# Attention on one core: a weave that starts with the second query tile, first rows loaded in f32 by the hardware queues, and a new order in the last period

## The chip, the core and the metric

The kernel runs on one core of a Trainium2 chip. The metric is the device time of one execution in microseconds (us), lower is better. A profile shows the span from the first to the last instruction, which is about 2 us shorter than the device time of the same execution. All runs quoted here were in the fast state, with a mean granted TensorE clock (its share of full speed) of 0.994 to 1.000. Single executions of one kernel still scatter by a few us, so medians are given with the lowest and highest run.

Engines: PE does the matmuls, DVE and ACT work on vectors, POOL issues the casting loads (the "software queue"), and SP issues stores and transposing transfers (a "hardware queue"; ACT can issue to one too). PSUM is the memory that takes the results of PE, in banks. "Landed" means that all bytes of a transfer have arrived.

## The reference

```python
# q, k, v: (8, 2048, 512) float32
scores = np.matmul(q, k.transpose(0, 2, 1)) / np.sqrt(d_k)
attn_weights = special.softmax(scores, axis=-1).astype(np.float32)
return np.matmul(attn_weights, v)
```

## The kernel before

A batch has four query tiles of 512 queries, so there are 32 tiles. Inputs are cast to f16 during the load. Both matrix products use a scheme with seven block products instead of eight (Winograd's form of Strassen's method). It needs sums of blocks, which DVE computes ("k sums", "q sums", "v sums", "p sums"). In matmuls of 256 columns, a score tile costs 112 this way and 128 when plain. The values of a tile cost 112.

In the steady loop a period (28 steps, called slots) weaves the scores of tile g+1 with the values of tile g on PE. A short queue of pending sums, `background`, is worked off in certain slots. DVE works in the order in which the instructions were written, and every sum is an instruction in that order.

```python
def prefetch(g, slot):                 # steady loop: loads, transposes, sums of later tiles
    ...
        elif what[0] == "trans":
            dma_transpose(what[1], bb, c)      # a transposing transfer, issued by SP
        else:
            background.extend({"k": k_sums, "q": q_sums, "v": v_sums}[what[1]](bb, c))
    if background and slot % len(QORDER) in (0, 2, 3, 6):
        background.popleft()()
```

Before the loop, tiles 0 and 1 are computed plainly, with the values of tile 0 put in late:

```python
load("q", 0, 0, 2); load("k", 0, 0, 2)         # software queue, f32 -> f16 on the way
load("k", 0, 1);    load("k", 0, 2)
...                                            # 14 dummy matmuls, first transposes on PE
for kb in range(NKB):
    plain_tile(0, kb)
    ...
load("q", 0, 2); load("q", 0, 3)
pe_transpose("q", 0, 1)
p_sums(0, NG - 1)
for kb in range(NKB):
    plain_tile(1, kb)
    if kb == 3: dma_transpose("q", 0, 2)
    if kb == 4: dma_transpose("q", 0, 3)
    ...                                        # v sums, p sums, first values of tile 0
for n in range(4, len(ORDER)):
    pv(0, n)                                   # the other values of tile 0, with k and q sums
    ...
for g in range(1, NP + 1):                     # the steady loop, first scores: tile 2
    ...
```

Each pair of output rows (`Pair`, letters a and b) goes through seven products. ACT scales a product into the output (`scaled`) and DVE adds to it (`final`). The pair's three PSUM banks are then free for the next pair. Lines are cut where "..." stands.

The softmax here doesn't subtract the row's maximum and nothing guards it: scores larger than these inputs give would overflow.

Of the kernel before, what the change touches and what calls it, by code (L numbers as in the profile page):

```python
# [12 lines left out]
def kernel(  # L13
# [21 lines left out]
    nc = tc.nc  # L35
# [49 lines left out]
    nc.sync.dma_start(out=ident[:], in_=ident_dram.ap())  # L85
# [12 lines left out]
    def load(what, b, c, pieces=1):  # L98
        t = stage.tile([P, CH, D], F16, tag="stage")
        w = CH // pieces  # L100
        for n in range(0, CH, w):
            at = c * CH + n
            nc.gpsimd.dma_start(out=t[:, n:n + w, :], in_=srcs[what][b, :, at:at + w, :])  # L103
        staged[what, b, c] = t
# [16 lines left out]
    def pe_transpose(what, b, c):  # L121
        src = staged.pop((what, b, c))
        t = operands(what)
        for n in range(0, CH, 2):
# [6 lines left out]
            nc.vector.tensor_copy(out=t[0][:, n:n + 2], in_=tr[:])  # L131
        (kT if what == "k" else qT)[b, c] = t
# [83 lines left out]

    class Group:
# [69 lines left out]
    def p_sums(g, n, part=None):  # L287
# [4 lines left out]
        if part in (None, 0):  # L292
            add(s1[:, js], a21, a22)  # L293
            sub(s2[:, js], s1[:, js], a11)  # L294
            sub(a21, a11, a21)
        if part in (None, 1):
            sub(s4[:, js], a12, s2[:, js])  # L297

    class Pair:
# [6 lines left out]
        def product(self, n):  # L306
# [3 lines left out]
            cols = slice(i * P, (i + 1) * P)  # L310
            if n == 1:
                self.x = bank("px")
            elif n == 2:
                self.y = bank("py")
            elif n == 5:
                self.z = bank("pz")
# [29 lines left out]
        def store(self, o, half):  # L346
            b, qt = divmod(self.g, NQT)
            n = qt * NQS + half * (NQS // 2) + self.i
            nc.sync.dma_start(out=out[b, n * P:(n + 1) * P, :], in_=o[:])
# [27 lines left out]
        def after7(self):  # L377
            self.final(self.o2[:, H:D], self.x[:, 0:H], self.r2)

        def after4(self):  # L380
            self.scaled(self.o2[:, 0:H], self.x[:, 0:H], self.r2)
            self.store(self.o2, 1)
# [30 lines left out]
    def prefetch(g, slot):  # L413
        b, qt = divmod(g, NQT)
        todo = PLAN.get((qt, slot), [])
        if g == 1:
            todo = [x for x in PLAN.get((0, slot), ()) if x[0] == "newv" or x[1] == "v"] + todo
        for what in todo:
            bb, c = b + 1, what[-1]
            if what[0] != "newv" and what[1] == "q":  # L420
                if not NQT <= g + what[2] < B * NQT:
                    continue
# [11 lines left out]
        if background and slot % len(QORDER) in (0, 2, 3, 6):  # L434
            background.popleft()()

# [4 lines left out]
    def pv(g, n):  # L441
        which = ORDER[n]
        g -= which.endswith("'")
        if g < 0:
            return
# [6 lines left out]
    load("q", 0, 0, 2)  # L452
    load("k", 0, 0, 2)
    load("k", 0, 1)
    load("k", 0, 2)

    dummy = bank("qy")
    for n in range(14):
        nc.tensor.matmul(dummy[:], warm[:, 0:P], warm[:], start=True, stop=True)
    pe_transpose("q", 0, 0)  # L460
    pe_transpose("k", 0, 0)
    new_v(0)
    load("k", 0, 3)
    load("q", 0, 1)
    for kb in range(NKB):
        plain_tile(0, kb)
        if kb % CH == 1 and kb // CH + 1 < NCH:
            pe_transpose("k", 0, kb // CH + 1)
        if kb % (2 * G) == 0 and kb:
            p_sums(0, kb // (2 * G) - 1)  # L470
        if kb % CH == 3:
            load_v(0, kb // CH)
    load("q", 0, 2)
    load("q", 0, 3)
    pe_transpose("q", 0, 1)
    p_sums(0, NG - 1)
    for kb in range(NKB):
        plain_tile(1, kb)
        if kb == 3:
            dma_transpose("q", 0, 2)  # L480
        if kb == 4:
            dma_transpose("q", 0, 3)
        if kb in (6, 8, 10, 11):
            for f in v_sums(0, (6, 8, 10, 11).index(kb)):
                f()
        if kb % (2 * G) == 0 and kb:
            p_sums(1, kb // (2 * G) - 1)
        if kb in (11, 15):
            pv(0, kb // 4 - 2)
        if kb in (13, 14):  # L490
            pv(0, kb - 11)
    p_sums(1, NG - 1)
    for n in range(4, len(ORDER)):
        pv(0, n)
        if n < 8:
            background.extend(k_sums(0, n - 4))
        if n == 8:
# [62 lines left out]
```

## Time and profile before

Three executions took a median of 817.41 us (815.86 to 817.48).

The first lines of the page of the kernel before, then its chain of waits by engine, and the transposing transfers (operation, count, median us from issue to landing):

```profile
span 814.3 us, 18274 instructions
PE 800.5 (98%) x7182; PEld 698.9 (86%) x7182; DVE 586.7 (72%) x1461; ACT 559.6 (69%) x1041; POOL 74.3 (9%) x118
...
PE 91%; DMA 4%; DVE 3%; ACT 1%; issue 0%; POOL 0%; ACTq 0%; DVEq 0%; POOLq 0%
...
raw<-t SPq DMA_TRANSPOSE x58, 5.3
```

PE is busy almost throughout. Only its gaps and its work can be cut. The view of waits on PE, kernel before (who waited, for whom; us in total, times, longest):

```profile
PE t L331 <- ACT o L339: 3.4, 6, 1.4
PE tr L128 <- DMA t<-in_k_dram: 2.2, 3, 1.3
PE t L331 <- DVE o L342: 1.4, 2, 0.8
PE t L459 <- DVE warm L451: 1.2, 1, 1.2
PE t L209 <- DVE raw L131: 0.9, 1, 0.9
PE tr L128 <- DMA t<-in_q_dram: 0.6, 1, 0.6
```

L331 is the value products, L250 the fast score products and L209 the plain score tiles. The timeline of the kernel before, cut to the instructions that mark borders (start, us, engine, line, operation, tiles, shape, count, idle time before it):

```profile
29.84 1.47 PE L209 MATMUL t<-raw 128*128 128x512 f16 x6 [0.94 <-DVE raw L131]
...
57.54 0.60 PE L250 MATMUL t<-raw 128*128 128x256 f16 x4
...
809.48 1.03 PE L331 MATMUL t<-t,right 128*128 128x256 f16 x8 [0.57 <-DVE o L342]
...
810.55 0.47 ACT L339 ACTIVATE o<-t,r 128x256 f32<-128x256 f32 x1 [2.73 <-PE t L331]
```

Three of these starts cut the execution: at tile 1's first scores (29.84), at tile 2's first scores (57.54) and at the end of the last matmul (810.55, when ACT takes its result). In the steady stretch groups of eight matmuls of 256 columns start 0.87 us apart, so one takes 0.109. (A timeline shows such a group as 1.03 or 1.04 us, from its first start to its last end.)

The issue view from 15 to 62 us shows what the two transposing transfers of q2 and q3 (query tiles 2 and 3) took:

```profile
raw<-t SPq DMA_TRANSPOSE x2, 18.8
```

That is 18.8 us, where the median of the page is 5.3. The loads of the next batch run at the same time.

### The profile page before, as it was taken

To read this page: it belongs to the slowest core of one execution; us is meant where nothing else is said; L and a number is where in the kernel's file an instruction comes from. 1 tells how busy PE (TensorE), PEld (TensorE's weight loads), DVE (VectorE), ACT (ScalarE), POOL (GpSimd) and SP (SyncE) were. 2 spreads that over 40 slices of the span, in tenths; PEclk is the share of its full clock that TensorE was granted. 3 is DMA by queue.
4 is the path that set the end of the run, shared out by engine and by line. 5 is a ranking of instruction groups with operands and counts; after the bars stand their busy time and mean duration, and the time that the engine had idled before them with its cause. 6 is when DMAs were issued, how large, how long until landed. Compare 5 with 4: busy or idle time off the path is not lost.

```text
span 814.3 us, 18274 instructions
## 1 busy us (share of the span) xinstructions
PE 800.5 (98%) x7182; PEld 698.9 (86%) x7182; DVE 586.7 (72%) x1461; ACT 559.6 (69%) x1041; POOL 74.3 (9%) x118
## 2 busy tenths in 40 slices
PE   8989999999999999999999999999999999999997
PEld 4468888888888888888888888888888888888886
DVE  3676877877866877677786777777777877766653
ACT  2636677677676777677777777776777776777772
POOL 5200003000020000200002000020002001000000
PEclk9999999999999999999999999999999999999999
DMA  9998863999659894797929979299982999721112
GB/s 161 206 162 181 144 133 80 208 188 143 124 108 206 155 169 102 118 224 148 173 67 155 220 144 147 75 178 188 169 153 66 194 181 178 148 67 40 53 40 78
DMA packets 190022, 115.51 MB, mean 142 GB/s; under 512 B 124400, under 2 KB 173552, under 8 KB 189936
## 3 DMA queue, kind: packets, MB, share of 16 engines
q0 software_dynamic: 50720, 50.34, 40.7%
q1 hardware_dynamic: 139216, 64.01, 36.9%
q8 instruction: 56, 0.92, 0.5%
q14 instruction: 30, 0.25, 0.1%
HBM read 100.70 MB, written 33.55 MB: 165 GB/s over the span
## 4 chain that ended last, share of the span: by engine, by line
PE 91%; DMA 4%; DVE 3%; ACT 1%; issue 0%; POOL 0%; ACTq 0%; DVEq 0%; POOLq 0%
PE t L331 45%; PE t L250 44%; DMA out_dram<-o 3%; PE t L209 2%; DMA t<-in_k_dram 1%; ACT o L339 0%; PE tr L128 0%; POOL t L103 0%; ACT left L199 0%; DVE s L293 0%; DVE o L342 0%; DVE s L294 0%; DVE s L297 0%; ACT right L199 0%; ACT t L263 0%
## 5 line engine op out<-in xcount | busy, mean ns | idle before, releaser
L339 ACT ACTIVATE o<-t,r 128x256 f32<-128x256 f32 x256 | 122.0, 477 | 142.4 <-DVE r L359 100.1
L250 PEld LDWEIGHTS <-raw 128*128 128x128 f16 x1920 | 187.9, 98 | 21.8
L250 PE MATMUL t<-raw 128*128 128x256 f16 x1440 | 196.6, 273 | 0.0
L199 ACT ACTIVATE left<-t 128x512 f16<-128x512 f32 (+1 forms) x272 | 157.5, 582 | 37.2 <-PE t L209 21.9
L331 PEld LDWEIGHTS <-s 128*128 128x128 f16 x1536 | 150.1, 98 | 23.1 <-issue 4.1
L250 PEld LDWEIGHTS <-ks 128*128 128x128 f16 x1440 | 140.9, 98 | 17.0 <-issue 0.7
L342 DVE SCALAR_TENSOR_TENSOR o<-t,r,o 128x256 f32<-128x256 f32 x192 | 92.3, 481 | 79.0 <-PE t L331 47.6
L331 PE MATMUL t<-t,s 128*128 128x257 f16 (+1 forms) x1024 | 133.2, 273 | 1.4 <-ACT o L339 1.4
L250 PE MATMUL t<-qs,ks 128*128 128x256 f16 x960 | 134.2, 273 | 0.1
L331 PE MATMUL t<-vh,left 128*128 128x256 f16 x1024 | 132.7, 273 | 0.0
L199 ACT ACTIVATE right<-cz 128x1024 f16<-128x1024 f32 x120 | 128.3, 1069 | 1.1 <-DVE cz L273 1.1
L267 ACT COPY cz<-t 128x512 f32<-128x512 f32 x120 | 70.4, 587 | 66.9 <-PE t L250 66.9
L331 PEld LDWEIGHTS <-right 128*128 128x128 f16 x1024 | 100.1, 98 | 14.4 <-issue 2.8
L331 PEld LDWEIGHTS <-left 128*128 128x128 f16 x1024 | 100.2, 98 | 11.8
L273 DVE TENSOR_TENSOR cz<-t,cz 128x512 f32<-128x512 f32 x120 | 82.4, 687 | 34.1 <-PE t L250 34.1
L276 DVE TENSOR_TENSOR cz<-t,cz 128x512 f32<-128x512 f32 x120 | 81.9, 683 | 1.9 <-PE t L250 1.9
L293 DVE TENSOR_TENSOR s<-right 128x512 f16<-128x512 f16 x128 | 53.9, 421 | 36.3 <-ACT right L199 31.8
L250 PE MATMUL t<-qs,raw 128*128 128x256 f16 x480 | 72.0, 273 | 0.0
L250 PE MATMUL t<-raw,ks 128*128 128x256 f16 x480 | 72.0, 273 | 0.0
L270 ACT COPY cz<-t 128x512 f32<-128x512 f32 x120 | 70.8, 590 | 0.0
L263 ACT COPY t<-t 128x512 f32<-128x512 f32 x120 | 68.4, 570 | 3.0
L331 PE MATMUL t<-vh,s 128*128 128x257 f16 x512 | 66.7, 273 | 1.6 <-ACT o L339 1.5
(38 smaller groups left out, 629.6 us busy)
## 6 DMA issues: line engine op xcount, KB each, us to landing
out_dram<-o SPq DMA_DIRECT2D x128, 256.0 KB, 3.8
vh<-in_v_dram POOLq DMA_DIRECT2D x32, 512.0 KB, 17.4
t<-in_k_dram POOLq DMA_DIRECT2D x31, 512.0 KB, 8.8
t<-in_q_dram POOLq DMA_DIRECT2D x31, 512.0 KB, 11.8
raw<-t SPq DMA_TRANSPOSE x58, 5.3
t<-in_q_dram POOLq DMA_DIRECT2D x2, 256.0 KB, 4.7
t<-in_k_dram POOLq DMA_DIRECT2D x2, 256.0 KB, 6.7
ident<-attn_identity SPq DMA_DIRECT2D x1, 32.0 KB, 1.6
```

The costliest lines, as they stand in the source:

```text
L199: nc.scalar.activation(out=out_, in_=in_, func=EXP, scale=inv_sqrt_d)
L209: nc.tensor.matmul(st[:], kT[b, c][0][:, n, dc, :], qT[b, qt][0][:, :, dc, :], start=(dc == 0), stop=(dc == ND - 1),)
L250: nc.tensor.matmul(dst[:, j * QH:(j + 1) * QH], lhs[:, j, c, :], rhs[:, :, c, :], start=(n in (1, 5) and j == 0 and c == 0), stop=(c == 1) ...
L263: nc.scalar.copy(out=self.y[:], in_=self.x[:])
L267: nc.scalar.copy(out=self.cz[:, :, 1, :], in_=self.two(self.z))
L270: nc.scalar.copy(out=self.cz[:, :, 0, :], in_=self.two(self.x))
L273: nc.vector.tensor_add(self.cz[:, :, 1, :], self.two(self.x), self.cz[:, :, 1, :])
L276: nc.vector.tensor_add(self.cz[:, :, 0, :], self.two(self.z), self.cz[:, :, 0, :])
L293: add(s1[:, js], a21, a22)
L331: nc.tensor.matmul(dst[:, 0:width], lhs(j), rhs(j), start=(first and j == 0), stop=(j == NJ - 1), skip_group_check=True,)
L339: nc.scalar.activation(out=out_, in_=src, func=COPY, scale=r[:])
L342: nc.vector.scalar_tensor_tensor(out=out_, in0=src, scalar=r[:], in1=out_, op0=MULT, op1=ADD)
```

## The change

Its intent is to start the woven loop one tile earlier (tile 1 becomes a fast tile, woven with the values of tile 0), to have the first rows sooner, and to take the waits out of the last period. The diff is cut to its core ("..." marks cuts; some calls are joined on a line, and most comments are added here):

```diff
+    def load_first(what, n, queue, room):          # a row tile in f32, no cast
+        ...
+        queue.dma_start(out=room, in_=srcs[what][0, :, n, :])
+    def round_first(what, n):                      # f32 -> f16 on DVE (q) or ACT (k)
+        f = nc.vector.tensor_copy if what == "q" else nc.scalar.copy
+        f(out=staged[what, 0, 0][:, n, :], in_=firsts[what, n])
...
-    load("q", 0, 0, 2)
-    load("k", 0, 0, 2)
-    load("k", 0, 1)
+    load_first("q", 0, nc.sync, row());   load_first("k", 0, nc.scalar, row())
+    load_first("q", 1, nc.sync, row());   load_first("k", 1, nc.scalar, row())
+    load_first("q", 2, nc.sync, rest[0]); load_first("q", 3, nc.sync, rest[1])
+    load_first("k", 2, nc.sync, rest[2]); load_first("k", 3, nc.sync, rest[3])
+    gate = const.tile([P, 1], F32)                 # software loads wait for k's first row
+    nc.gpsimd.tensor_copy(out=gate[:], in_=firsts["k", 0][:, 0:1])
+    load("k", 0, 1, (2, 2))
...
-    for kb in range(NKB):
-        plain_tile(1, kb)
-        ...
+    FIRST = "a1 b1 a5 a3 a2 a6 a7 b5 a4 b3 b2 b6".split()
+    LAST = "b7' a1 b4' a5 b1 a3 b5 a6 b3 a2 b6 a7 b7 a4 b2 b4".split()
...
-    for g in range(1, NP + 1):
+    for g in range(NP):
...
         # in prefetch
+        if g == 0:
+            todo = [x for x in todo if x[0] != "newv" and x[1] == "q"]
+            if slot == 2:
+                dma_transpose("q", 0, 2)
+            if slot == 9:
+                dma_transpose("q", 0, 3)
...
-                if not NQT <= g + what[2] < B * NQT:
+                if not (2 if what[0] == "sum" else NQT) <= g + what[2] < B * NQT:
...
-        if background and slot % len(QORDER) in (0, 2, 3, 6):
+        if background and (g == 0 or slot % len(QORDER) in (0, 2, 3, 6)):
             background.popleft()()
+            if background and ((g == 0 and slot in (0, 1, 8, 10, 12, 14, 15, 16, 17, 18)) or ...):
+                background.popleft()()
...
         # class Pair: the last pair b has PSUM banks of its own and stores in halves
+            self.apart = g == NP - 1 and i == 1
+            own = "q" if self.apart else "p"
```

Not shown: tile 0's first scores are computed in halves of 256 queries, and the p, k and v sums of the start join `background`. In the first period the q sums of tile 2 now enter that queue at slot 12, behind the remaining k and v sums.

More of the change, by code (lines that the diff above doesn't have):

```diff
@@ L84 @@
     ident_dram = nc.inline_tensor(np.eye(P, dtype=np.float16), name="attn_identity")
-    nc.sync.dma_start(out=ident[:], in_=ident_dram.ap())
+    nc.scalar.dma_start(out=ident[:], in_=ident_dram.ap())
     qT, kT = {}, {}
@@ L96, with load @@
     }
-    def load(what, b, c, pieces=1):
-        t = stage.tile([P, CH, D], F16, tag="stage")
-        w = CH // pieces
-        for n in range(0, CH, w):
+    def load(what, b, c, pieces=(CH,)):
+        t = staged.get((what, b, c))
+        if t is None:
+            t = staged[what, b, c] = stage.tile([P, CH, D], F16, tag="stage", name="stage")
+        n = CH - sum(pieces)
+        for w in pieces:
             at = c * CH + n
             nc.gpsimd.dma_start(out=t[:, n:n + w, :], in_=srcs[what][b, :, at:at + w, :])
-        staged[what, b, c] = t
+            n += w
+    firsts = {}
+    def load_first(what, n, queue, room):
+        if (what, 0, 0) not in staged:
+            staged[what, 0, 0] = stage.tile([P, CH, D], F16, tag="stage", name="stage")
+        firsts[what, n] = room
+        queue.dma_start(out=room, in_=srcs[what][0, :, n, :])
+    def round_first(what, n):
+        f = nc.vector.tensor_copy if what == "q" else nc.scalar.copy
+        f(out=staged[what, 0, 0][:, n, :], in_=firsts[what, n])
     def operands(what):
@@ L119, in dma_transpose, with pe_transpose @@
         (kT if what == "k" else qT)[b, c] = t
-    def pe_transpose(what, b, c):
-        src = staged.pop((what, b, c))
-        t = operands(what)
-        for n in range(0, CH, 2):
+    def pe_transpose(what, b, c, n0=0, n1=CH):
+        src = staged[what, b, c]
+        if n0 == 0:
+            (kT if what == "k" else qT)[b, c] = operands(what)
+        t = (kT if what == "k" else qT)[b, c]
+        for n in range(n0, n1, 2):
             tr = psum["px"].tile([P, 2, ND, P], F16, tag="px", name="tr")
@@ L130, in pe_transpose @@
                     )
-            nc.vector.tensor_copy(out=t[0][:, n:n + 2], in_=tr[:])
-        (kT if what == "k" else qT)[b, c] = t
+            if n and c:
+                nc.scalar.copy(out=t[0][:, n:n + 2], in_=tr[:])
+            else:
+                nc.vector.tensor_copy(out=t[0][:, n:n + 2], in_=tr[:])
+        if n1 == CH:
+            staged.pop((what, b, c))
     def k_blocks(t):
@@ L215, in plain_tile, with plain_half @@
         exp(right[:, kb // 2, kb % 2, :], st[:, QH:QTW])
+    def plain_half(g, j, half):
+        b, qt = divmod(g, NQT)
+        if j == 0 and half == 0:
+            new_p(g)
+        st = bank("qx")
+        kt, qt_ = kT[b, j // G][0], qT[b, qt][0]
+        for s in range(2):
+            for dc in range(ND):
+                nc.tensor.matmul(
+                    st[:, s * QH:(s + 1) * QH], kt[:, 2 * (j % G) + s, dc, :],
+                    qt_[:, 2 * half:2 * half + 2, dc, :],
+                    start=(s == 0 and dc == 0), stop=(dc == ND - 1), skip_group_check=True,
+                )
+        left, right, _ = pts[g]
+        if half:
+            exp(right[:, j], st[:].rearrange("p (s q) -> p s q", s=2))
+        else:
+            for s in range(2):
+                exp(left[s][:, j, :], st[:, s * QH:(s + 1) * QH])
     class Group:
@@ L285, in exp_right, with p_sums @@
             exp(self.right[:, self.js], self.cz[:])
-    def p_sums(g, n, part=None):
+    def p_sums(g, n):
         left, right, (s1, s2, s4) = pts[g]
@@ L291, in p_sums @@
         a12, a22 = left[1][:, js], right[:, js, 1]
-        if part in (None, 0):
-            add(s1[:, js], a21, a22)
-            sub(s2[:, js], s1[:, js], a11)
-            sub(a21, a11, a21)
-        if part in (None, 1):
-            sub(s4[:, js], a12, s2[:, js])
+        return [
+            lambda: add(s1[:, js], a21, a22),
+            lambda: sub(s2[:, js], s1[:, js], a11),
+            lambda: sub(a21, a11, a21),
+            lambda: sub(s4[:, js], a12, s2[:, js]),
+        ]
     class Pair:
@@ L313, in product @@
             elif n == 2:
-                self.y = bank("py")
+                self.y = bank(own + "y")
             elif n == 5:
-                self.z = bank("pz")
+                self.z = bank(own + "z")
             lhs, rhs, dst = {
@@ L344, in final, with store @@
             )
-        def store(self, o, half):
+        def store(self, o, half, ds=slice(0, D)):
             b, qt = divmod(self.g, NQT)
             n = qt * NQS + half * (NQS // 2) + self.i
-            nc.sync.dma_start(out=out[b, n * P:(n + 1) * P, :], in_=o[:])
+            nc.sync.dma_start(out=out[b, n * P:(n + 1) * P, ds], in_=o[:, ds])
         def store_first(self):
@@ L378, in after7 @@
             self.final(self.o2[:, H:D], self.x[:, 0:H], self.r2)
+            if self.apart:
+                self.store(self.o2, 1, slice(H, D))
         def after4(self):
             self.scaled(self.o2[:, 0:H], self.x[:, 0:H], self.r2)
-            self.store(self.o2, 1)
+            self.store(self.o2, 1, slice(0, H if self.apart else D))
     ORDER = "a1 b7' a5 b4' a3 b1 a6 a2 a7 b5 a4 b3 b2 b6".split()
@@ L415, in prefetch @@
         todo = PLAN.get((qt, slot), [])
-        if g == 1:
+        if g == 0:
[4 more added lines that the diff above has]
+                dma_transpose("q", 0, 3)
+        elif g == 1:
             todo = [x for x in PLAN.get((0, slot), ()) if x[0] == "newv" or x[1] == "v"] + todo
@@ L433, in prefetch, with pv @@
                 background.extend({"k": k_sums, "q": q_sums, "v": v_sums}[what[1]](bb, c))
-        if background and slot % len(QORDER) in (0, 2, 3, 6):
+        if background and (g == 0 or slot % len(QORDER) in (0, 2, 3, 6)):
             background.popleft()()
+            if background and ((g == 0 and slot in (0, 1, 8, 10, 12, 14, 15, 16, 17, 18)) or (0 < g < NQT and slot % 14 == 6)):
+                background.popleft()()
     NP = B * NQT
     pairs = {}
-    def pv(g, n):
-        which = ORDER[n]
+    def pv(g, which):
         g -= which.endswith("'")
-        if g < 0:
-            return
         if which[1] == "1":
@@ L451, with row @@
     nc.vector.memset(warm[:], 0.0)
-    load("q", 0, 0, 2)
-    load("k", 0, 0, 2)
-    load("k", 0, 1)
+    def row():
+        t = opool.tile([P, D], F32, tag="o", name="first")
+        return t[:]
+    rest = [czpool.tile([P, G, 2, QH], F32, tag="cz", name="cz") for _ in range(2)]
+    rest = [t[:, j].rearrange("p s q -> p (s q)") for t in rest for j in range(2)]
+    load_first("q", 0, nc.sync, row())
+    load_first("k", 0, nc.scalar, row())
+    load_first("q", 1, nc.sync, row())
+    load_first("k", 1, nc.scalar, row())
@@ L455 @@
+    load_first("q", 2, nc.sync, rest[0])
+    load_first("q", 3, nc.sync, rest[1])
+    load_first("k", 2, nc.sync, rest[2])
+    load_first("k", 3, nc.sync, rest[3])
+    gate = const.tile([P, 1], F32)
+    nc.gpsimd.tensor_copy(out=gate[:], in_=firsts["k", 0][:, 0:1])
+    load("k", 0, 1, (2, 2))
     load("k", 0, 2)
+    new_v(0)
+    load_v(0, 0)
     dummy = bank("qy")
-    for n in range(14):
-        nc.tensor.matmul(dummy[:], warm[:, 0:P], warm[:], start=True, stop=True)
-    pe_transpose("q", 0, 0)
@@ L461, with idle @@
-    pe_transpose("k", 0, 0)
-    new_v(0)
+    def idle(n):
+        for _ in range(n):
+            nc.tensor.matmul(dummy[:], warm[:, 0:P], warm[:], start=True, stop=True)
+    idle(11)
+    for n in range(2):
+        round_first("q", n)
+        round_first("k", n)
+    pe_transpose("q", 0, 0, 0, 2)
+    idle(2)
+    pe_transpose("k", 0, 0, 0, 2)
+    idle(2)
+    for n in range(2, 4):
+        round_first("q", n)
+        round_first("k", n)
+    pe_transpose("q", 0, 0, 2, 4)
+    plain_half(0, 0, 0)
@@ L463, with both @@
+    pe_transpose("k", 0, 0, 2, 4)
+    plain_half(0, 0, 1)
+    plain_half(0, 1, 0)
+    pe_transpose("k", 0, 1, 0, 2)
+    plain_half(0, 1, 1)
     load("k", 0, 3)
     load("q", 0, 1)
-    for kb in range(NKB):
+    for c in range(1, NCH):
+        load_v(0, c)
+    def both(c):
+        return [f for fs in zip(k_sums(0, c), p_sums(0, c)) for f in fs]
+    background.extend(both(0))
+    for kb in range(2 * G, NKB):
         plain_tile(0, kb)
+        if kb == 4:
+            pe_transpose("k", 0, 1, 2, 4)
@@ L467 @@
         if kb % CH == 1 and kb // CH + 1 < NCH:
             pe_transpose("k", 0, kb // CH + 1)
-        if kb % (2 * G) == 0 and kb:
-            p_sums(0, kb // (2 * G) - 1)
-        if kb % CH == 3:
-            load_v(0, kb // CH)
+        if kb == 12:
+            pe_transpose("q", 0, 1)
+        for _ in range(2):
+            if background:
+                background.popleft()()
+        if kb % CH == 3 and kb // CH + 1 < NCH:
+            background.extend(both(kb // CH))
+        if kb == 13:
+            background.extendleft(reversed(q_sums(0, 1)))
@@ L473 @@
     load("q", 0, 2)
     load("q", 0, 3)
-    pe_transpose("q", 0, 1)
-    p_sums(0, NG - 1)
-    for kb in range(NKB):
-        plain_tile(1, kb)
-        if kb == 3:
-            dma_transpose("q", 0, 2)
-        if kb == 4:
-            dma_transpose("q", 0, 3)
-        if kb in (6, 8, 10, 11):
-            for f in v_sums(0, (6, 8, 10, 11).index(kb)):
-                f()
-        if kb % (2 * G) == 0 and kb:
-            p_sums(1, kb // (2 * G) - 1)
-        if kb in (11, 15):
-            pv(0, kb // 4 - 2)
-        if kb in (13, 14):
-            pv(0, kb - 11)
@@ L492 @@
-    p_sums(1, NG - 1)
-    for n in range(4, len(ORDER)):
-        pv(0, n)
-        if n < 8:
-            background.extend(k_sums(0, n - 4))
-        if n == 8:
-            background.extend(q_sums(0, 2))
-            background.extend(q_sums(0, 3))
-        if background:
-            background.popleft()()
-            background.popleft()()
+    background.extend(p_sums(0, NG - 1))
+    of_v = [f for fs in zip(*(v_sums(0, c) for c in range(NCH))) for f in fs]
+    background.extend(of_v[:NCH])
@@ new lines, with after_slot @@
+    background.extend(of_v[2 * NCH:3 * NCH])
+    background.extend(k_sums(0, NCH - 1))
+    background.extend(of_v[NCH:2 * NCH])
+    background.extend(of_v[3 * NCH:])
+    FIRST = "a1 b1 a5 a3 a2 a6 a7 b5 a4 b3 b2 b6".split()
+    LAST = "b7' a1 b4' a5 b1 a3 b5 a6 b3 a2 b6 a7 b7 a4 b2 b4".split()
+    def after_slot(g):
+        if g == 0:
+            return {n: [(g, x)] for n, x in zip([9, 11, 13, 15, 17, 18, 19, 21, 23, 25, 26, 27], FIRST)}
+        return {2 * n + 1: [(g, x)] for n, x in enumerate(LAST if g == NP - 1 else ORDER)}
@@ L504 @@
     prev = None
-    for g in range(1, NP + 1):
-        for slot in range(NS):
+    for g in range(NP):
+        todo = after_slot(g)
+        for slot in range(NS + 4):
             n, at = divmod(slot, len(QORDER))
             old, what = QORDER[at]
-            if g + 1 < NP:
-                if at == 0:
-                    cur = Group(g + 1, n)
-                if old == 0:
-                    cur.product(what)
-            if old == 1 and prev is not None:
-                prev.product(what)
-            if prev is not None:
-                if at == 2:
-                    prev.exp_right()
-                if at == 4:
-                    p_sums(prev.g, prev.n, 0)
-                if at == 5:
-                    p_sums(prev.g, prev.n, 1)
-            if at == len(QORDER) - 1:
-                prev = cur if g + 1 < NP else None
-            if slot % 2 == 1:
-                if g < NP or ORDER[slot // 2].endswith("'"):
-                    pv(g, slot // 2)
-            if g < NP:
+            if slot < NS:
+                if g + 1 < NP:
+                    if at == 0:
+                        cur = Group(g + 1, n)
+                    if old == 0:
+                        cur.product(what)
+                if old == 1 and prev is not None:
+                    prev.product(what)
+                if prev is not None:
+                    if at == 2:
+                        prev.exp_right()
+                    if at == 4:
+                        for f in p_sums(prev.g, prev.n)[:3]:
+                            f()
+                    if at == 5:
+                        p_sums(prev.g, prev.n)[3]()
+                if at == len(QORDER) - 1:
+                    prev = cur if g + 1 < NP else None
+            for x in todo.get(slot, ()):
+                pv(*x)
+            if slot < NS:
```

## The prediction

> **What bounds it.** PE. The page gives PE 98% busy of 814.3 us, and the chain of waits puts 91% on PE. In the steady stretch eight 256-column matmuls take 0.873 us (timeline), so one costs 0.109 us; from 70 to 790 us no gap longer than 0.2 us shows. Counting matmuls: 30 fast score tiles x 112 + two plain ones x 128 + 32 x 112 for the values = 7200, or 786 us, and 96 transposes at 0.055 us make 5 us. So about 22 us are not useful PE work. By counts in stretches: 16 before 71 us, 2.4 in the last 20 us before the last matmul (waits of 0.4 to 0.6 us on ACT and DVE), 3.8 after it (ACT, then the last store of 256 KB).
>
> In the first part: idle or dummy work to 6.2 us; waits for q and k halves (landed 5.9, 7.2, 9.3, 10.5 us) and for k's second chunk (13.1); 1.3 us at 28.5; and some 6 us between 45 and 66.6, partly DVE/ACT chains, partly DMA: the transfers stay saturated to about 57 us, the two transposing transfers of q take 18.8 us each instead of about 4.7, the first store behind them 10.4, and ACT waits 4.4 us for it until 65.
>
> **What changes.**
> 1. Query tile 1 becomes a fast tile: 16 matmuls of 256 columns fewer, -1.75 us. Certain.
> 2. Rows of q and k in f32 by hardware queues. The Trainium skill, "DMA: Bandwidth & Descriptors", section "SWDGE vs HWDGE vs iDMA", says a cast needs the software queue; hence new roundings on DVE and ACT. The same page says all queues share 16 engines. The trace agrees on sharing: 1 MB of f32 lands every 2.6 us however issued. So the first 2 MB should land near 7.5 us instead of 10.5, and all later loads some 3 us earlier. Plain tile 0 ends (with q1 transposed) near 26.5 us instead of 29.8: about -3.3.
> 3. Tile 1's scores are woven with tile 0's values. Removes DVE/ACT chains at 45-56, but puts 24 background sums plus q sums into a 22 us period: DVE nearly full (about 23 us by 0.39 us a sum, 0.68 an addition).
> 4. That does not remove the DMA backlog: I expect q2 to land near 31, its transpose near 47-50 (18.8 us, same contention). In the DVE's order q2's sums stand before additions PE needs, so DVE, then PE, wait there: 3 to 8 us, eating much of what steps 2 and 3 won. Then the second full period starts at 52 to 57 us instead of 57.5, and stores still wait behind the transposes.
> 5. Last period: own PSUM banks for the second pair, half stores: -1.5 to -2.5 us of tail.
>
> Added: 8 roundings, at most 0.7 us each (DVE's PSUM copy of 1024 columns takes 0.69), mostly beside transfers.
>
> **Prediction.** The useful work and fixed ends would allow a span near 801; with the DMA wait I expect 807 and, with the 3 us between span and median, 809.5 us. Range 803.5 to 814. Faster by over 2% (below 801): 5%; within 2%: 93%; slower by over 2%: 2%. Gain about 1%.
>
> **What shows it.** First real transposes at 5-6 us and first scores near 8; k's second chunk at about 10; plain tile done at 26-27; waits table with a DVE wait on the transposed q near 45-50 followed by PE waiting on a DVE addition; ACT waiting for a store near 60; steady 0.873 us per eight matmuls unchanged; last 20 us with under 1 us of PE waits.
>
> **What would make it wrong.** The transposing transfer may land by 42 us (then 803-806); f32 loads may be slower than 400 GB/s; DVE overload may stall PE in the first period; the second PSUM pair may bring waits of its own.

## The result and the profile after

Four executions of the changed kernel took a median of **815.87 us** (815.11 to 816.69); four of the kernel before, in the same rounds, took 816.63 us (815.46 to 817.48). The ratio is 0.9992 with a 95% interval of 0.9973 to 1.0011: no difference that these runs can tell. Here and below, a ratio is the mean time of one kernel's runs over that of the other's of the same rounds, so it is not quite the ratio of the medians. The predicted range ended at 814.0, so the result lies outside it.

The same lines of the page of the kernel after. The profiled execution is its fastest, at 815.11 us:

```profile
span 813.1 us, 18448 instructions
PE 798.7 (98%) x7247; PEld 705.8 (87%) x7247; DVE 589.6 (73%) x1473; ACT 570.6 (70%) x1039; POOL 72.1 (9%) x116
...
PE 93%; DMA 5%; POOL 0%; ACT 0%; issue 0%; DVE 0%; ACTq 0%; POOLq 0%
...
raw<-stage SPq DMA_TRANSPOSE x58, 6.2
```

And its waits on PE (L375 are now the value products, L292 the fast score products, L383 ACT's `scaled`):

```profile
PE t L292 <- DVE cz L318: 5.2, 1, 5.2
PE tr L145 <- ACT stage L119: 1.6, 1, 1.6
PE t L375 <- ACT o L383: 1.2, 1, 1.2
PE t L529 <- DVE warm L502: 1.2, 1, 1.2
PE tr L145 <- DVE stage L119: 1.0, 2, 0.7
PE t L292 <- ACT t L305: 0.4, 1, 0.4
```

The waits for ACT's and DVE's output work fell from 4.8 us to 1.2. In their place stands one single wait of 5.2 us. The chain of waits in order of time (start, us, what) shows where it comes from:

```profile
1.63 6.05 DMA first<-in_k_dram
...
16.79 16.59 DMA stage<-in_q_dram
33.38 0.02 issue
33.40 18.14 DMA raw<-stage
51.54 0.02 issue
51.56 0.42 DVE qs L181
51.98 0.61 DVE cz L318
52.60 0.04 issue
52.64 1.01 PE t L292 x4
```

Read it downwards. Tile q2's load lands at 33.4. Its transposing transfer takes 18.1 us. At once a DVE sum of q2 (`qs`) follows, then an addition that has nothing to do with q2 (`cz`, of tile 1's scores), and then PE. DVE's timeline shows why PE hung on q2 at all:

```profile
45.02 0.41 DVE L210 TENSOR_TENSOR t<-vh,t 128x512 f16<-128x512 f16 x1
51.56 0.42 DVE L181 TENSOR_TENSOR qs<-raw 128x512 f16<-128x512 f16 x1 [6.13 <-DMA raw<-stage]
51.90 0.68 DVE L318 TENSOR_TENSOR cz<-t,cz 128x512 f32<-128x512 f32 x1
```

The q sum stood at the head of DVE's queue for 6.13 us, and the addition behind it could not pass. The Trainium skill, "TensorE: Matmul & The Clock Gate", in the first table ("Engine queue depth"), says that the queues of ScalarE, VectorE and GpSimdE (here ACT, DVE and POOL) are strictly first in, first out. The traces agree: here the addition started at 51.90 us, 0.34 us after the q sum; in e2 below, where the q sums stand later in DVE's order, the same addition started at 45.26.

PE's timeline, kernel after:

```profile
28.57 0.60 PE L292 MATMUL t<-raw 128*128 128x256 f16 x4
...
46.80 0.60 PE L292 MATMUL t<-raw 128*128 128x256 f16 x4
52.64 1.01 PE L292 MATMUL t<-qs,ks 128*128 128x256 f16 x4 [5.24 <-DVE cz L318]
53.45 1.92 PE L375 MATMUL t<-t,right 128*128 128x256 f16 x8
...
59.66 1.04 PE L292 MATMUL t<-raw 128*128 128x256 f16 x8
...
809.70 0.47 ACT L383 ACTIVATE o<-t,r 128x256 f32<-128x256 f32 x1 [1.27 <-PE t L375]
```

Eight matmuls shown as 1.04 us before the wait are shown as 1.92 right after it. The stretches (us, busy time of each engine, granted clock, DMA share, GB/s) name the reason:

```profile
48.00:52.00 4.00, 0.00 (x0) 0.00 (x0) 0.44 (x2) 0.00 (x0) 0.00 (x0) 1.00 1.22 196
52.00:56.00 4.00, 3.36 (x19) 2.49 (x19) 3.04 (x8) 1.85 (x3) 0.74 (x1) 0.57 1.26 180
56.00:60.00 4.00, 4.00 (x39) 3.58 (x38) 2.68 (x7) 2.68 (x7) 0.10 (x1) 1.00 1.37 178
```

From 52 to 56 us the granted clock was 0.57. The 40 matmuls from 52.64 to 58.35 took 5.71 us instead of 4.37 at 0.109 each, so the wait cost 1.3 us more after it had ended. The Trainium skill, same page, section "Part 1: The HAM clock gate", says that PE falls to half clock after an idle window of about 3.4 us and that this window runs freely. The trace agrees: PE stood idle for 5.24 us, and by single microseconds the granted clock was 1.00 until 52 us and 0.50 from 52 to 55.

With the borders of both timelines the whole difference can be set out. Lost time is the length of a stretch less 0.109 us per matmul:

| stretch (us) | before | after | what changed |
|---|---|---|---|
| start to tile 1's first scores | 29.84 | 28.57 | -1.3, head |
| to tile 2's first scores | 27.70 | 31.09 | work 24.5 to 21.9 (224 to 200 matmuls); lost 3.2 to 9.2 |
| to the end of the last matmul | 753.01 | 750.04 | work +0.9 (8 matmuls of tile 1 come here); lost 3.8 less |
| to the end | 3.75 | 3.40 | -0.35, half stores |
| span | 814.3 | 813.1 | |

So the changes did win time: 1.75 us of work, 1.3 at the head, and some 4 after tile 2's first scores. The second stretch lost 6.0 us more than before, and that took nearly all of it back.

### The profile page after: what moved, and what is told of

Same layout as the page of the kernel before. It is cut to its first block, busy times and chain, and to the rows that moved or that the text cites. A ratio compares the mean times of both kernels' runs of the same rounds, so it can differ in the third digit from the quotient of the medians.

```text
span 813.1 us, 18448 instructions
## 1 busy us (share of the span) xinstructions
PE 798.7 (98%) x7247; PEld 705.8 (87%) x7247; DVE 589.6 (73%) x1473; ACT 570.6 (70%) x1039; POOL 72.1 (9%) x116
## 4 chain that ended last, share of the span: by engine, by line
PE 93%; DMA 5%; POOL 0%; ACT 0%; issue 0%; DVE 0%; ACTq 0%; POOLq 0%
PE t L375 48%; PE t L292 46%; DMA raw<-stage 2%; DMA stage<-in_q_dram 2%; DMA first<-in_k_dram 1%; POOL vh L199 0%; PE tr L145 0%; ACT o L383 0%; PE t L247 0%; POOL stage L105 0%; DVE raw L151 0%; ACT left L220 0%; ACT stage L119 0%; DVE cz L318 0%; ACTq L115 0%
## 5 line engine op out<-in xcount | busy, mean ns | idle before, releaser
L383 ACT ACTIVATE o<-t,r 128x256 f32<-128x256 f32 x256 | 122.2, 477 | 134.8 <-DVE r L403 113.4
L292 PEld LDWEIGHTS <-raw 128*128 128x128 f16 x1984 | 194.1, 98 | 22.8
L292 PE MATMUL t<-raw 128*128 128x256 f16 x1488 | 203.0, 273 | 0.0
L375 PEld LDWEIGHTS <-s 128*128 128x128 f16 x1536 | 150.3, 98 | 19.7 <-issue 1.4
L292 PEld LDWEIGHTS <-ks 128*128 128x128 f16 x1488 | 145.8, 98 | 23.5 <-issue 6.2
L292 PE MATMUL t<-qs,ks 128*128 128x256 f16 x992 | 139.4, 273 | 5.7 <-DVE cz L318 5.2
L220 ACT ACTIVATE right<-cz 128x1024 f16<-128x1024 f32 x124 | 132.6, 1069 | 1.5 <-DVE cz L315 1.5
L375 PE MATMUL t<-t,s 128*128 128x257 f16 (+1 forms) x1024 | 133.1, 273 | 0.0
L375 PE MATMUL t<-vh,left 128*128 128x256 f16 x1024 | 132.7, 273 | 0.0
L309 ACT COPY cz<-t 128x512 f32<-128x512 f32 x124 | 72.7, 586 | 67.3 <-PE t L292 67.0
L375 PEld LDWEIGHTS <-right 128*128 128x128 f16 x1024 | 100.6, 98 | 12.6 <-issue 0.6
L375 PEld LDWEIGHTS <-left 128*128 128x128 f16 x1024 | 100.2, 98 | 11.6
L315 DVE TENSOR_TENSOR cz<-t,cz 128x512 f32<-128x512 f32 x124 | 85.1, 686 | 33.9 <-PE t L292 33.9
L318 DVE TENSOR_TENSOR cz<-t,cz 128x512 f32<-128x512 f32 x124 | 84.7, 683 | 2.4 <-PE t L292 2.2
L292 PE MATMUL t<-qs,raw 128*128 128x256 f16 x496 | 74.4, 273 | 0.0
L292 PE MATMUL t<-raw,ks 128*128 128x256 f16 x496 | 74.4, 273 | 0.0
L312 ACT COPY cz<-t 128x512 f32<-128x512 f32 x124 | 73.2, 590 | 0.2 <-PE t L292 0.2
L305 ACT COPY t<-t 128x512 f32<-128x512 f32 x124 | 70.7, 570 | 3.3 <-ACT o L383 0.3
L375 PE MATMUL t<-vh,s 128*128 128x257 f16 x512 | 66.8, 273 | 1.2 <-ACT o L383 1.2
```

The source lines that it names most:

```text
L220: nc.scalar.activation(out=out_, in_=in_, func=EXP, scale=inv_sqrt_d)
L292: nc.tensor.matmul(dst[:, j * QH:(j + 1) * QH], lhs[:, j, c, :], rhs[:, :, c, :], start=(n in (1, 5) and j == 0 and c == 0), stop=(c == 1) ...
L305: nc.scalar.copy(out=self.y[:], in_=self.x[:])
L309: nc.scalar.copy(out=self.cz[:, :, 1, :], in_=self.two(self.z))
L312: nc.scalar.copy(out=self.cz[:, :, 0, :], in_=self.two(self.x))
L315: nc.vector.tensor_add(self.cz[:, :, 1, :], self.two(self.x), self.cz[:, :, 1, :])
```

## The experiments

The theory was that the loads of the next batch hold up q2's transposing transfer, and that DVE's fixed order carries this wait to PE. Rivals were that PE is held by DVE's amount of work, that the head is limited by the software loads, or that the clock alone is to blame. Every kernel was run in five rounds beside the kernel before, and all were correct. Edits are against the changed kernel unless said otherwise.

### The next batch's loads held until the transposes have landed (e1)

```diff
     # in prefetch, first lines
+        if g == 1 and slot == 0:
+            for qt_ in (2, 3):
+                nc.gpsimd.tensor_copy(out=gate[:], in_=qT[0, qt_][0][:, 0, 0, 0:1])
```

POOL, which issues those loads, copies one element of each transposed tile first, and so waits for both.

> Changed kernel, but the software loads of the next batch (and of the fourth query tile after) wait until the transposes of q2 and q3 have landed. Theory A (q2's transposing transfer is slow because it shares the engines with loads nobody needs yet, and DVE then PE wait for it): the transpose of q2 takes 5 to 9 us instead of 18.1 and lands before 43 us, DVE's wait of 6.1 us and PE's of 5.2 us go, the clock does not fall, span 806 to 808, time about 809, ratio to before 0.990 to 0.993. Theory B (DVE has too much background work in the first period): nothing moves, span 813. Theory C (a transposing transfer is slow in itself this early): transpose still 15 us or more.

Measured: 808.79 us (808.52 to 810.77), against 816.18 for the kernel before; ratio 0.9909 (0.9888 to 0.9931). The two transposes took 5.9 and 4.4 us, with the issue at 33.2 us almost unchanged. PE's waits from 28 to 60 us in this run:

```profile
PE t L375 <- ACT o L383: 1.2, 1, 1.2
PE t L292 <- ACT t L305: 0.4, 1, 0.4
```

The wait of 5.2 us is gone. Cut at the same borders, the span of 806.5 us is 28.72, then 24.37, then 750.04, then 3.4. The third stretch is equal to that of the changed kernel to the last digit, and the second is 6.7 us shorter. The wait (5.2) and the slow clock after it (1.3) make 6.5 of this. The contention theory held. The Trainium skill, "DMA: Bandwidth & Descriptors", section "SWDGE vs HWDGE vs iDMA", subsection "Issuing engines are not separate DMA queues", says that transfers of all issuing engines run on the same 16 DMA engines and interleave. The runs agree in so far as loads that POOL issues slow a transfer that SP issues, and they add the size: about 5 us with the loads held, about 18 us beside them.

### The transposes as slow as they are, but q2's sums at the end of DVE's period (e2)

```diff
-                if not (2 if what[0] == "sum" else NQT) <= g + what[2] < B * NQT:
+                if not (3 if what[0] == "sum" else NQT) <= g + what[2] < B * NQT:
     # in the loop
+            if g == 0 and slot == NS - 1:
+                for f in q_sums(0, 2):
+                    f()
```

> Changed kernel with the four sums of q2 moved from the middle of the first period to its end in DVE's order; all transfers as they were. Theory A in its narrow form (the harm is the place of these sums ahead of additions that PE needs, not the late landing): q2's transpose still lands at 51 to 52 us after some 18 us, DVE does not wait for it before 50 us, PE's wait of 5.2 us goes, span 806 to 808. If the late landing itself is the limit: PE waits about as long, some microseconds later, span 812 to 813. Theory B (DVE overload): span 812 to 813 with DVE busy and PE waiting on it.

Measured: 808.92 us (808.49 to 813.37), ratio 0.9925 (0.9897 to 0.9952), and a span of 806.5. The issue view from 15 to 62 us shows that the transfers did not get faster:

```profile
raw<-stage SPq DMA_TRANSPOSE x2, 18.6
```

PE's wait for DVE is gone all the same: from 28 to 100 us its only waits are the two of e1, 1.2 and 0.4 us. So a slow transfer alone costs nothing here. It hurts because a sum that needs it stands ahead of an addition that PE needs. Either cure removes the loss. Both cures leave all of DVE's sums in place, so its amount of work is not what made the 5.2 us.

### q2 transposed on PE instead (e3)

```diff
-            if slot == 2:
-                dma_transpose("q", 0, 2)
     # and e2's first change; pe_transpose takes the PSUM bank as its last argument
+            if slot == 14:
+                pe_transpose("q", 0, 2, 0, 2, "py")
+            if slot == 16:
+                pe_transpose("q", 0, 2, 2, 4, "py")
+                background.extend(q_sums(0, 2))
```

> Changed kernel with q2 transposed on PE in the first period instead of by a transfer (16 more PE transposes, about 0.9 us; two more copies on DVE and ACT). Theory A: no wait on a transposing transfer, span about 807 to 809 (6.5 us won, 0.9 us and some waits on the copies paid). Theory B: 813 or more, since DVE gets more work still.

Measured: 812.07 us (811.22 to 815.43), ratio 0.9955 (0.993 to 0.998). This wins about half and misses its expectation (a span of 807 to 809; the profiled one is 811.6). PE needs no transfer now, but it waits for ACT, which copies the transposed tile out of PSUM behind its other work. PE's timeline in this run:

```profile
44.10 1.03 PE L375 MATMUL t<-vh,left 128*128 128x256 f16 x8 [2.24 <-ACT raw L149]
```

And the stretch from 44 to 48 us (columns as above):

```profile
44.00:48.00 4.00, 3.90 (x25) 3.01 (x25) 2.37 (x7) 1.60 (x4) 0.00 (x0) 0.67 1.21 196
```

A wait of only 2.24 us was followed by a clock of 0.67 from 44 to 48 us (and 0.90 from 48 to 52). This run also lost 0.9 us near 700 us in a wait that comes up again below.

### The new last period alone, on the kernel before (e4)

The edit moves only `LAST`, the second pair's own banks and the half stores into the kernel before:

```diff
+            self.apart = g == NP - 1 and i == 1
+            own = "q" if self.apart else "p"
...
-                self.y = bank("py")
+                self.y = bank(own + "y")
...
+    LAST = "b7' a1 b4' a5 b1 a3 b5 a6 b3 a2 b6 a7 b7 a4 b2 b4".split()
```

> Kernel before with only the new last period (order, own banks for the second pair, half stores). If the last period is worth what the traces say (waits of 2.4 us before the last matmul fall to 0.1, and 3.8 us after it to 3.4): span 811 to 812, 2.5 us less than before, ratio 0.996 to 0.998. If it is worth nothing: ratio 1.000.

Measured: 813.35 us (813.12 to 814.75), against 816.18; ratio 0.9967 (0.9946 to 0.9988). PE has no wait after 57 us in the profiled run. The last period's part of the change is worth 2.8 us by medians, a little more than predicted. Some of it may not be its own: the profile of the kernel before also has a wait of 0.5 us near 65 us, which this edit does not touch and which did not come in this run.

### The f32 rows taken out again, with e1's gate (e5)

```diff
-    load_first("q", 0, nc.sync, row())
-    ...                                   # all eight rows, their gate and roundings
+    load("q", 0, 0, (2, 2))
+    load("k", 0, 0, (2, 2))
     # and the gate of e1; the small identity matrix is loaded from SP's queue again, not ACT's
```

> e1 (next batch's loads held back) with the first q and k chunks loaded as in the kernel before: cast by the software queue in halves, no f32 rows, no roundings, no gate on the first software loads. If the f32 rows by hardware queues are worth what was forecast: span 808.5 to 810 against 806.5 of e1 (first scores 2 to 3 us later). If they buy next to nothing (the traces show first scores at 10.5 us with them and 11.0 without): span 806 to 807.5.

Measured: 810.31 us (808.13 to 811.08), ratio 0.9921 (0.9905 to 0.9937). The executions are of two kinds: two at a mean clock of 1.000 took 808.1 to 808.2 us, and four at 0.998 took 810.3 to 811.1. The profiled one is of the first kind; its span is 806.4 us against e1's 806.5, and its first scores start at 9.85 us. In the changed kernel they start at 10.46 (before: 10.99). So at equal clock, in the one profile of each, eight rows by hardware queues bought nothing over halves by the software queue. What may speak for them is that e1 had the slower kind only once in six.

### All software loads held until the last f32 row (e6)

```diff
-    nc.gpsimd.tensor_copy(out=gate[:], in_=firsts["k", 0][:, 0:1])
+    nc.gpsimd.tensor_copy(out=gate[:], in_=firsts["k", 3][:, 0:1])
     # and the gate of e1
```

> e1, and the first software loads wait for the last f32 row of k instead of the first. If the f32 rows land late (9.4 us) because software loads share the engines from 6.5 us on: last row lands by 8.5 us, first scores near 9.6, span 805.5 to 806 against 806.5. If the rows are limited by their own rate: no change of the last row's landing, k's second chunk lands 2 to 3 us later (13 to 14 us), span 806.5 to 808.

Measured: 812.65 us (812.08 to 812.76), ratio 0.9953 (0.994 to 0.9966), slower than e1. With nothing from the software queue beside them the f32 rows landed no sooner: k's second row took 7.1 us from its issue, where it took 6.05 in the changed kernel. So it is not the software loads that hold them up. Why it took longer still is not shown. From 3 to 8 us the eight rows in flight moved 289 to 395 GB/s with no software load beside them; the lowest and the highest stretch (columns as above):

```profile
5.00:6.00 1.00, 1.00 (x11) 0.66 (x10) 0.43 (x1) 0.42 (x1) 0.00 (x0) 1.00 0.93 289
7.00:8.00 1.00, 0.00 (x0) 0.00 (x0) 0.00 (x0) 0.00 (x0) 0.00 (x0) 1.00 1.03 395
```

The profiled span of 810.5 us misses both expected ones: first scores came at 11.77 us, and from 12 to 16 us the granted clock was 0.58. The software queue read 1 MB of f32 per 2.6 us, or 403 GB/s, in the kernel before. The Trainium skill, "DMA: Bandwidth & Descriptors", section "Where 436 GB/s comes from", gives 435 GB/s for the fabric and about 358 GB/s for the memory of one core. The software loads lie above the second of these numbers and below the first.

### e1's gate in the kernel before (e7)

```diff
     # and the tile `gate`; in prefetch, first lines
+        if g == 1 and slot == 0:
+            for qt_ in (2, 3):
+                nc.gpsimd.tensor_copy(out=gate[:], in_=qT[0, qt_][0][:, 0, 0, 0:1])
```

> Kernel before, with only the gate of e1 (next batch's loads wait for the transposes of q2 and q3). The same contention stood in the kernel before, but PE waited less on it: ACT's wait of 4.4 us for a store and DVE's of 2.2 us for q3 should go; PE's part in this is some 1 to 2 us. Span 812 to 813.5 against 814.3, ratio 0.997 to 0.999. If the contention cost the kernel before as much as the changed one: span below 810.

Measured: 815.67 us (815.04 to 817.85), ratio 0.9996 (0.9982 to 1.0011). The median transpose fell from 18.8 to 5.9 us, as the issue view from 30 to 62 us shows:

```profile
raw<-t SPq DMA_TRANSPOSE x2, 5.9
```

The time did not move clear of the noise; the expected gain (a ratio of 0.997 to 0.999) is neither shown nor excluded. The contention was there before the change, but little that PE needed stood behind it: in the profile of the kernel before, a first store took 10.4 us, ACT waited 4.4 us for it, and PE 0.5 us for ACT near 65 us. The change created the dependence that costs 5.2 us, not the contention.

### The wait filled with dummy matmuls (e8)

```diff
+            if g == 0 and slot == 22:
+                fill = bank("py")
+                for _ in range(22):
+                    nc.tensor.matmul(fill[:], warm[:, 0:P], warm[:], start=True, stop=True)
```

> Changed kernel with 22 dummy matmuls of 512 columns (4.8 us) on PE just where it waits 5.2 us for the addition behind q2's sums. They should take the place of the idle time, so that the granted clock does not fall after it. After the wait the changed kernel needed 1.3 us more than at full clock (8 matmuls in 1.7 us for 0.87). If the clock's fall is a cost of its own: span 811.5 to 812.2 against 813.1. If not: 813 or more.

Measured: 817.51 us (815.21 to 819.81), ratio 1.0015 (0.9995 to 1.0035). The time went against the expectation. In the profiled run three other things went wrong: the head lost clock (tile 1's first scores at 30.89), the dummies ran about 2 us past the landing of q2 (51.9), and PE waited 1.9 us near 700 us. As a test by time it is inconclusive. Within the trace it does answer the question it was made for. PE's timeline from 50 us on (the window cuts off the first of the 22 dummies):

```profile
49.78 4.70 PE L621 MATMUL t<-warm 128*128 128x512 f16 x21
54.31 0.60 PE L292 MATMUL t<-qs,ks 128*128 128x256 f16 x4
54.75 1.04 PE L375 MATMUL t<-t,right 128*128 128x256 f16 x8
...
58.69 0.60 PE L292 MATMUL t<-raw 128*128 128x256 f16 x4
```

The same 40 matmuls took 4.38 us (54.31 to 58.69) instead of 5.71, at a granted clock of 1.00 from 52 to 60 us. The 1.3 us after the wait was the slow clock.

### Four attempts at the rest (e9 to e12)

Kernel e9 is e1 with nine dummy matmuls instead of two after q's first transposes, against early falls of the clock.

> e1 with 9 instead of 2 dummy matmuls between the first transposes of q and those of k, where PE sat idle 1.6 to 2.6 us for k's second row. Some executions of e1, e2, e5 and e8 are 2 to 3 us longer at a mean granted clock of 0.998; the profile of e8 shows the clock at half from 10 to 13.7 us. If that early fall of the clock, set off by the idle time, makes these executions: all runs near 808.6, none over 809.5, mean clock 1.000. If not: one or more in six stays at 810 or more.

Measured: 810.33 us (808.65 to 810.98), ratio 0.9924 (0.99 to 0.9947). The mean clock was now 1.000 in six of six, and yet four of the six took 810 us or more: the expectation failed. DVE's timeline shows another wait of the same kind, late in the run:

```profile
698.98 0.42 DVE L170 TENSOR_TENSOR ks<-raw 128x512 f16<-128x512 f16 x1 [2.59 <-DMA raw<-stage]
```

It is k's transposing transfer, which took 17.3 us with two q loads issued beside it. PE waited 1.4 us. Such a wait (0.2 to 3.0 us on DVE) is in the profiled runs of the changed kernel, e3, e6, e8, e9, e11 and e12. It is not in those of the kernel before, e1, e2, e4, e5, e7 and e10.

Kernel e10 is e9 with fewer double pops in the first period, to test whether the sums that stand on DVE ahead of a reciprocal hold PE.

```diff
-            ... (g == 0 and slot in (0, 1, 8, 10, 12, 14, 15, 16, 17, 18)) ...
+            ... (g == 0 and slot in (0, 1, 14, 15, 16, 17, 18, 19)) ...
```

> e9 with three background sums fewer in DVE's order ahead of the first reciprocal of the first period (they come later). In the changed kernel and e1, PE waits 1.2 us there for ACT, ACT for that reciprocal. If it waits because DVE is full of sums (the rival theory of overload, in the small): this wait falls to 0.3 us or less and the span by 0.5 to 1.2 us, 805.5 to 806. If not, or if the sums are missed later: 806.5 or more.

Measured: 809.86 us (808.05 to 814.39), ratio 0.9928 (0.9897 to 0.9959). PE's wait for ACT's output fell from 1.2 to 0.3 us and the profiled span to 805.8. So the sums that stand ahead on DVE are a true cause of this small wait, worth about 0.9 us in the profile. By medians it can't be told from the scatter.

Kernel e11 is e9 with only the first two rows of q and k in f32, and the other two by the software queue at once.

> e9 with only rows 0 and 1 of q and k in f32 by hardware queues, rows 2 and 3 of each by software loads issued at once, no gate on the first software loads. If k's second row is late (7.7 us) because eight rows share the engines: it lands by 6 us, first scores at 8.5 to 9.5 us instead of 10.5, span 805 to 806. If the first 2 MB take their time however they are issued: first scores still at 10 us or later, span 806.5.

Measured: 810.99 us (808.02 to 814.07), ratio 0.993 (0.9901 to 0.9959). Tile 1's first scores started at 28.13 us, 0.8 us before e9's, and k's second row still landed at 7.67 (changed kernel: 7.68). Replacing half of the f32 rows by software loads did not bring the others sooner, and what it won is small.

Kernel e12 is e10 with the sums of k's last chunk three slots later, against the wait near 700 us.

```diff
-        (2, 14, "load", "k", 3), (2, 27, "trans", "k", 3), (3, 11, "sum", "k", 3),
+        (2, 14, "load", "k", 3), (2, 27, "trans", "k", 3), (3, 14, "sum", "k", 3),
```

> e10 with the sums of k's last chunk three slots later in DVE's order in every batch. The profiles of e3, e8 and e9 show the same wait once more near 700 us, in the last batch: DVE waits 2.0 to 3.0 us for a transposing transfer of k, PE 0.9 to 1.9 us for the addition behind it; e1, e2, e5 and e10 were free of it in their profiles. If this wait makes the executions at 809.5 to 811 us with a clock of 1.000: it shrinks, five of six executions lie at 807.5 to 808.8, ratio to before 0.989 to 0.991. If they come from elsewhere: the spread of e9 and e10 stays (808 to 810.5).

Measured: 808.52 us (808.3 to 811.16), ratio 0.9912 (0.9897 to 0.9927). Four of six executions took 808.3 to 808.6 us. The profiled one took longer, and it still has DVE waiting 2.5 us for k's transpose and PE 1.3. So three slots were not enough, and what decides in which executions that wait comes is left open. Kernels e1, e2, e5 and e9 to e12 all beat the kernel before, by 0.7 to 0.9%, and their intervals overlap, so they can't be told apart. The changed kernel did not run in the same rounds.

## Why the prediction was wrong, point by point

The prediction gave 809.5 us as the sum of a span of 801 that "useful work and fixed ends would allow", 6 us for the DMA wait, and some 3 us between span and time. The profiled span was 813.1. Kernel e1 lacks exactly the wait, so the two terms can be measured one by one.

- **The bound.** Right: PE is 98% busy, and eight steady matmuls still take 0.87 us.
- **Step 1, 16 fewer matmuls, -1.75 us.** This held by count (224 to 200 matmuls in the second stretch, 8 of them moved to the third).
- **Step 2, the head, -3.3 us.** This failed: -1.3 us. The first real transposes came at 5.05 us, as expected, but the first scores only at 10.46 us instead of 8, because k's second row landed at 7.68. That is 0.5 us sooner than before; most of the other 0.8 us is the wait of 0.9 us for DVE before tile 1, which went. k's second chunk was issued in halves near 5.2 and 5.9 us and took a median of 6.1 us, so it was there at about 11 to 12 us instead of 10 (before: 13.0), but PE no longer waited for it. The assumption "1 MB of f32 lands every 2.6 us however issued" was read from software loads alone; e6 shows the rows to be slow by themselves, and in e5's profile they bought nothing.
- **Step 3, the removed DVE/ACT chains.** This is the largest error. The prediction gives no figure for this step, but its sum of 801 contains about 6 us for it (814.3 less 1.75, 3.3 and 2 for the tail, down to 801), and it counted "some 6 us between 45 and 66.6" as lost. From 45.66 to 66.59 us the kernel before did 152 matmuls, 16.6 us of work, in 20.9 us: 4.3 us were lost there. The kernel before lost only 3.2 us in tile 1's stretch, and e1 still loses 2.5 there, 1.6 of it in waits for ACT that the denser schedule brings. About 1.3 us more was won after tile 2's first scores (3.8 and 0.35, less the 2.8 of the tail), among it the wait of 0.5 us near 65 us. That makes 2 us instead of 6.
- **Step 4, the DMA wait, 3 to 8 us.** The mechanism and the place were right. The transpose took 18.1 us, close to what was read from the kernel before, DVE waited at 45 to 51.6 us, and PE behind it. q2 landed at 33.4 us instead of 31, only 1.1 us sooner than before (its transpose was issued at 34.45), much as the head. The wait cost 6.6 us of span (813.1 less 806.5), where the prediction's sum has 6: 5.2 of waiting and 1.3 of slow clock, which the prediction did not name. That the total comes so close is in part luck. The sign "ACT waiting for a store near 60" did not come: no such wait is in the profile after.
- **Step 5, the tail, -1.5 to -2.5 us.** Right, slightly more: -2.8 us by e4.

Without the wait, then, the change won 7.8 us (814.3 to 806.5) where the prediction's sum had 13.3. The head is short by 2.2 us (e1: -1.1) and the removed chains by about 4; the tail gave 0.8 more. The failed step is the base of 801, made of steps 2 and 3, not the wait: a real cost was foreseen and then set against gains that were 5.5 us too large. A gain of about 1% was forecast; 0.1% was measured, which the runs can't tell from none.

The chance of 93% for "within 2%" was borne out. The warning that "f32 loads may be slower than 400 GB/s" was the one that came true; "DVE overload" did in a small way, with about 0.9 us in one profile (e10).

Two things stay open: the wait for k's transpose near 700 us, which comes in some executions only, and why the f32 rows moved no faster than 289 to 395 GB/s. At these rates the eight rows, 2.1 MB, take 5.3 to 7.3 us by an estimate from e6, so the late rows took about the time that all eight need together.

## What to carry to other kernels

An in-order engine turns a late transfer into a wait of everything behind it. Place an instruction that depends on a DMA behind those that the bottleneck needs, or hold back the transfers that compete, and ask for each transfer whether its time was read alone or under load. When a removed wait is counted as a gain, count no more than what the stretch takes beyond its useful work, and subtract what the new schedule will itself wait for. Before netting a cost against gains, measure the gains without the cost, as the one-line gate did here: the change was worth 0.9% with the gate (which alone, in the kernel before, showed no gain), and a single ordering took it back.

## What the Trainium skill lacked or had wrong

- "DMA: Bandwidth & Descriptors" has no figure for a transposing transfer beside other loads. Here a 512 KB transpose took 4.4 and 5.9 us with the loads held (e1), and 17.8 to 19.4 us beside them (changed kernel, e2). Its table in "Latency and other measured facts" gives an effective 261 GB/s for a transpose with a non-contiguous middle dimension, with no word on load.
- The same page, in the section "Rules for kernel authors", says that spreading transfers over issuing engines does not help bandwidth. That held for the head (e5), but the page does not say that plain f32 rows by the hardware queues can be slower than casting loads by the software queue: 289 to 395 GB/s (e6) against 403 GB/s of f32 read (kernel before), and 6 to 7 us for the last of the eight 256 KB rows, against 2.9 us for the first.
- "TensorE: Matmul & The Clock Gate", Part 1, subsection "HAM oscillation — how this bites in real kernels", gives the abstract rule of no gaps above about 3.4 us. Part 1 also tells of a kernel in which frequent short idle times made the clock swing, but not how long they were. Here the clock fell after waits below 3.4 us: after one of 2.24 us (0.67 from 44 to 48 us, e3; it was still 1.00 from 44 to 45, when PE was at work again, and 0.50 from 46 to 48), and at the head of e6 after one of 2.62 us with shorter ones near it (0.58 from 12 to 16 us).
